# Moving the head transposes of the first attention block, its bias-table loads and its stored-value loads

## The chip, the cores and the metric

The kernel runs on one core of a Trainium2 chip. The metric is device microseconds of one execution, from the first instruction to the last result; 1697.91 us is the median of three runs of the kernel before (1692.98, 1697.91 and 1699.44).

## The reference

Two transformer blocks on one sequence of 512 tokens, 1024 features wide, each with a mixer and a feed-forward part. The part that the change touches is the first block's mixer, which adds two branches: an RWKV branch (a recurrence over the tokens) and a sparse attention with 8 heads in 2 key groups. Cut to that attention:

```python
q = rmsnorm(q.reshape(b, s, G, R, dh), q_norm_g) * (dh ** -0.5)
kc = rmsnorm(compress_blocks(k_c, ...), k_norm_g)          # 31 compressed keys
p_c = masked_softmax(einsum(q, kc) + bias_c, dist_c >= 0)  # compressed branch
o_cmp = einsum(p_c, vc)
# selected branch: rmsnorm(k_s); n_sel = min(16, 8 blocks): every causal block is selected
sc = einsum(q, k_sel) + bias; p = masked_softmax(sc, mask); o_slc = einsum(p, v_sel)
# window branch: rmsnorm(k_w), a window of 512 tokens
# output = gate_c * o_cmp + gate_s * o_slc + gate_w * o_win, then a projection,
# a sigmoid gate per feature, and the same for the RWKV branch
```

Queries and keys are normalised head by head, so a head's values must all be there, squared, summed and scaled, before they can be used. The second block has another attention (top-k over index scores) and a mixture of experts behind it.

## The kernel before

Everything is float32 with inputs in four tiles of 128 tokens. An exact product is made of three matmuls of rounded parts, hi by hi, hi by lo and lo by hi (`mm3`, L252). `wload` (L257) brings a 256 KB piece of a weight from memory on SP's queue (`raw`, 4 buffers), rounds it on ACT (`hi`, 3 buffers) and takes the rest on POOL or DVE (`lo`, 3 buffers).

A framework records the program and places the instructions of each engine in an order of its own, from the program order, the data that they need and the buffers of the pools; within an engine they then run strictly in that order. So the code's order is a wish: a transposition written behind a projection may already stand inside the next one.

`lin_a` (L268) projects the four token tiles at once, with weights as the moving operand: 8 steps of 128 features, 12 matmuls each, in four PSUM tiles (`pslin` twice, `pspr` twice). It takes a function `mid`, which is recorded once more than half of the steps are through. `lin_heads` (L1076) calls it and then normalises per head: ACT scales and squares, DVE sums, takes the reciprocal root in a row of small steps, and multiplies (the tiles are `hd` for keys, `hq` and `q` for queries). `lin_b` (L285) is the other form, weights stationary, 128x512 outputs; its rows are called dense below.

The first block's mixer is `block1`. After the RWKV recurrence come the gate products of tiles 8 to 15 (`gates`), then `nsa_in`: compressed keys and values, the RWKV output (`rwkv_out`, which ends in the tiles `obh`, `obl`), the q projection, the transposition of q's heads into `qT`, and for c = 0 (selected) and c = 1 (window) a projection of keys, values and gate (`w_kv`) and the transposition of two key groups into `kT`. Then `nsa_pair` runs four times, for one head of each group, called A and B: the compressed branch (scores in `CA`/`CB`, exponential on ACT, sums on DVE, four transposes, a product with `vc`), and two full branches: scores QK into `psA`/`psB` (two buffers each), bias and minimum on DVE (`NA`, `mnA`), exponential on ACT (`PA`), scaling by one over the sum on DVE, 10 transposes per head and products with `V`. The bias comes from a table `TB` per head (`toeplitz`, four DMAs on SP each). Work without that dependence fills the gaps: `proj_b` (dense, `obh`, `obl`, with `mb` made on DVE), `gates(range(8))` and behind them `merge`.

In the second block, `dsa_in` calls `lin_heads` for q and k, with `mid` for the transposition of q inside k's projection and of k inside v's, while DVE searches the top-k of the scores (`dsa_topk`); `dsa_pair` then runs its attention with heads A and B in step.

Of the kernel before, what the change touches and what calls it, by code (L numbers as in the profile page):

```python
# [10 lines left out]
F32 = mybir.dt.float32  # L11
F32R = mybir.dt.float32r
# [4 lines left out]
ALU = mybir.AluOpType  # L17
AX = mybir.AxisListType

T = 512  # L20
D = 1024
NT = 4
# [174 lines left out]
class Kern:  # L197
# [70 lines left out]
    def lin_a(self, pieces, h, N, consume, mid=None):  # L268
        ps = [self.pt("lin"), self.pt("lin"), self.pt("pr"), self.pt("pr")]
        kt, last = 0, sum(p.shape[-1] // N for p in pieces) - 1  # L270
        for p in pieces:
            hi, lo = self.wload(p)
            for j in range(p.shape[-1] // N):
                for t in range(NT):
                    c = slice(t * 128, (t + 1) * 128)
                    self.mm3(ps[t][:, :N], (h[0][:, kt, c], h[1][:, kt, c]),
                             (hi[:, j * N:(j + 1) * N], lo[:, j * N:(j + 1) * N]), kt == 0, kt == last)
                kt += 1
            if mid and kt > last // 2:
                mid()  # L280
                mid = None
        for t in range(NT):
            consume(t, ps[t])
# [126 lines left out]
    def block1(self):  # L410
        nc, tc, I = self.nc, self.tc, self.I
        with ExitStack() as s1:
            self.gt = s1.enter_context(tc.tile_pool(name="gt", bufs=1))
            self.thd = self.dr.tile([16, 128, T], F32, name="thd")
            self.bvd = self.dr.tile([4, 128, T], F32, name="bvd")
            self.ynd = self.dr.tile([NT, 2, 128, 256], F32, name="ynd")
            with tc.tile_pool(name="rw", bufs=1) as rw:
                self.rw = rw
                with tc.tile_pool(name="rwp", bufs=1, side="right") as rp:
                    self.rp = rp  # L420
                    with tc.tile_pool(name="nrm", bufs=1, side="right") as nrm, tc.tile_pool(name="btab", bufs=1) as bt:
                        self.rwkv_open(nrm, bt)
                    self.load_cc(rw, "cc1")
                    self.rwkv_in()
                    with tc.tile_pool(name="rwm", bufs=1, side="right") as rm:
                        self.rm = rm
                        for b in range(2):
                            for hp in range(2 * b, 2 * b + 2):
                                self.X[hp] = self.rwkv_col(hp, rw)
                                self.X[8 + hp] = self.rwkv_col(8 + hp, rw)  # L430
                                self.rwkv_prep(hp)
                            for t in range(NT):
                                self.rwkv_batch(t, b, ("A", "B", "pr")[(4 * b + t) % 3])
                        self.gates(range(8, 16))
            mx = s1.enter_context(tc.tile_pool(name="mx", bufs=1))
            self.mx = mx
            self.obT = (mx.tile([128, 4, T], F32R, name="obh"), mx.tile([128, 4, T], F32R, name="obl"))
            self.nsa_in()
            if self.stop == "nsa_in":
                return  # L440
            self.mb = s1.enter_context(tc.tile_pool(name="mbp", bufs=1)).tile([128, 8, T], F32, name="mb")
            with tc.tile_pool(name="att", bufs=1) as at:
                self.at = at
                for i in range(4):
                    pso = self.pt()
                    self.nsa_pair(i, pso)
                    self.split(pso, self.oaT[0][:, i, :], self.oaT[1][:, i, :])
                    self.dump("oaT", self.oaT[0][:, i, :].bitcast(F32), (slice(None), i))
                self.proj_b()
                self.gates(range(8))  # L450
            self.xs = self.rstack.enter_context(tc.tile_pool(name="xs", bufs=1, side="right"))
            self.x = self.xs.tile([128, NT, D], F32, name="x")
            nc.scalar.dma_start(self.x, I["x"].rearrange("(t p) d -> p t d", p=128))
            self.mtp = s1.enter_context(tc.tile_pool(name="mtp", bufs=1))
            self.merge()
            self.h_open("fg")
            self.ss = self.out_proj(I["w_o1"], self.mT, after=self.h_half)
            self.dump("x1", self.x)

    def nsa_in(self):  # L460
        nc, tc, I, mx = self.nc, self.tc, self.I, self.mx
# [9 lines left out]
        qs = mx.tile([128, 1], F32, name="qs")  # L471
        self.stt(qs, self.pc("qg"), -0.125, self.pc("kg"), ALU.mult, ALU.mult)
        self.load_cc(mx, "cc5")
        with tc.tile_pool(name="cmp", bufs=1) as cp:
# [59 lines left out]
                    self.split(pv, self.kcT[0][:, :, 0:31], self.kcT[1][:, :, 0:31], scale=qs)  # L534

            qt = self.lin_heads(cp, [I["w_q"][j] for j in range(8)], 512, 8)
            q2 = cp.tile([128, NT, 8, 2, 64], F32R, name="q2", tag="w1", bufs=1)
            for t in range(NT):
                self.split(qt[t], q2[:, t, :, 0], q2[:, t, :, 1])
            for h in range(8):  # L540
                ps = self.pt("AB"[h % 2])
                for t in range(NT):
                    self.tr(ps[:, t * 128:(t + 1) * 128], q2[:, t, h].rearrange("p j d -> p (j d)").bitcast(F32))
                self.copy("av"[h % 2], self.qT[:, h, :], ps)
            for c in range(2):

                def extra(t, ps):
                    self.copy("a", self.V[:, t, c, :], ps[:, 128:256])
                    self.act(self.gate[:, 3 - t, 12 * c:12 * c + 12], ps[:, 256:268], AF.Tanh, scale=0.5)

                kt = self.lin_heads(cp, [I["w_kv"][4 * c + j] for j in range(4)], 268, 2, extra, dup=True)
                for g in range(2):
                    ps = self.pt("AB"[g])
                    for t in range(NT):
                        self.tr(ps[:, t * 128:(t + 1) * 128], kt[t][:, g].rearrange("p j d -> p (j d)"))
                    self.split(ps, self.kT[0][:, c, g, :], self.kT[1][:, c, g, :], scale=qs)
            self.ts(self.gate, self.gate, 0.5, 0.5)

    def softmax_min(self, N, ps, tb, mn):
        self.nc.vector.tensor_tensor_reduce(out=N, in0=ps, in1=tb, scale=1.0, scalar=3.0e38,  # L560
                                            op0=ALU.add, op1=ALU.min, accum_out=mn)

    def nsa_pair(self, i, pso):
        nc, at = self.nc, self.at
# [2 lines left out]
        TB = []  # L567
        for g in range(2):
            h, tg = i + 4 * g, tl(g)
            tb3 = tg([128, 1, 896], "TB", 1)  # L570
            self.toeplitz(self.tab1, h, tb3)
            tb = tb3[:, 0, :]
            TB.append(tb)
            ps = self.pt("AB"[g])
            for t in range(NT):
# [391 lines left out]
    def rwkv_out(self):  # L967
        nc, tc = self.nc, self.tc
        with tc.tile_pool(name="rwo", bufs=1) as ro:
            bv = ro.tile([128, 4, T], F32, name="bv")  # L970
            nc.sync.dma_start(bv, self.bvd.rearrange("h p t -> p h t"))
            g2 = ro.tile([128, 512], F32, name="g2")
            nc.sync.dma_start(g2, self.I["g2"])
            mu1 = ro.tile([128, 1], F32, name="mu1b")
            self.ts(mu1, self.pc("mu", 13), -1.0, 1.0)
            ps = self.lin_b(self.I["w_rw"][13], self.h)
            x = ro.tile([128, T], F32, name="xl13")
            self.act(x, ps, AF.Identity, scale=mu1)
            self.stt(x[:, 1:], ps[:, :T - 1], self.pc("mu", 13), x[:, 1:], ALU.mult, ALU.add)
            self.act(x, x, AF.Tanh, scale=0.5)  # L980
            self.ts(x, x, 0.5, 0.5)
            for hp in range(4):
                yn = ro.tile([128, NT, 128], F32, name="yn", tag="yn", bufs=2)
                nc.sync.dma_start(yn, self.ynd[:, hp // 2, :, hp % 2 * 128:hp % 2 * 128 + 128].rearrange("t p c -> p t c"))
                ps = self.pt("A")
                for t in range(NT):
                    self.tr(ps[:, t * 128:(t + 1) * 128], yn[:, t, :])
                o = ro.tile([128, T], F32, name="otmp", tag="otmp", bufs=2)
                self.act(o, ps, AF.Identity, scale=self.pc("lg", hp), bias=self.pc("lb", hp))
                self.tt(o, o, bv[:, hp, :], ALU.add)  # L990
                ps = self.pt("B")
                self.mm(ps, g2[:, hp * 128:(hp + 1) * 128], x)
                self.tt(o, ps, o)
                self.split(o, self.obT[0][:, hp, :], self.obT[1][:, hp, :])
                self.dump("obT", o, (slice(None), hp))
# [722 lines left out]
```

## Time and profile before

| | us |
|---|---|
| median of three runs | 1697.91 |
| the profiled execution | 1697.58 |
| its span on the core | 1695.8 |
| PE busy | 1579.2 (93%) |
| DVE busy | 951.0 (56%) |
| ACT busy | 558.1 (33%) |
| mean granted TensorE clock | 0.955 |

The span runs from the first to the last instruction. Matmuls overlap, so PE counts as busy also where it runs at the lower of its two clocks: a granted clock of 1.00 is 2.4 GHz, 0.50 is 1.2 GHz, and a number between them is the mean over a stretch. Of the span, 384 to 640 us is the first block's projections and attention, 1110 to 1180 us the second block's projections, and the experts of the second block end it, behind loads from memory.

### The profile page before, as it was taken

How to read it: one execution, taken by the hardware profiler on the slowest of the kernel's cores; microseconds unless marked ns; L12 is line 12 of the kernel's file. 1: busy time of each engine (PE TensorE's matmuls, PEld its weight loads, DVE VectorE, ACT ScalarE, POOL GpSimd, SP SyncE). 2: the span in 40 equal slices, each digit the busy share in tenths (PEclk: the TensorE clock that was granted, in tenths of full speed). 3: DMA queues.
4: the chain of work that ended last, by engine and by line, in shares of the span. 5: the costliest groups of instructions: out<-in, count | busy, mean ns of one | idle time of the engine just before them, and what ended most of it. 6: DMA issues, size and time to landing. Idle time of an engine off the chain costs nothing. (4 is left out here: it accounts for less than half of the span.)

```text
span 1695.8 us, 25436 instructions
## 1 busy us (share of the span) xinstructions
PE 1579.2 (93%) x9595; PEld 1145.5 (68%) x9595; DVE 951.0 (56%) x2344; ACT 558.1 (33%) x1127; POOL 292.0 (17%) x232
## 2 busy tenths in 40 slices
PE   7999999998899999999999999989888996899995
PEld 5678787868566577888888888677666475465431
DVE  5566866136587542777777333798488635343310
ACT  3432322325244433444444232434333431011010
POOL 4510101523110144000000000132032031121111
PEclk8899999999799999999999999999999997899898
DMA  5110111632222253223333333423211368899995
GB/s 188 62 57 16 57 55 51 211 102 64 80 74 66 87 166 89 87 95 93 100 93 94 93 94 104 100 75 95 69 38 38 144 229 308 282 403 401 403 393 186
DMA packets 90760, 230.74 MB, mean 136 GB/s; under 512 B 16015, under 2 KB 20527, under 8 KB 82156
## 3 DMA queue, kind: packets, MB, share of 16 engines
q1 hardware_dynamic: 76608, 203.29, 35.2%
q0 software_dynamic: 4736, 11.14, 2.7%
q10 hardware_dynamic: 9292, 14.66, 2.6%
q8 instruction: 77, 1.26, 0.3%
q14 instruction: 47, 0.39, 0.1%
HBM read 217.49 MB, written 21.04 MB: 141 GB/s over the span
## 5 line engine op out<-in xcount | busy, mean ns | idle before, releaser
L227 ACT ACTIVATE hi<-raw 128x512 fp32r<-128x512 f32 (+1 forms) x314 | 197.4, 631 | 434.5 <-PE pslin L246 186.1
L215 POOL TENSOR_TENSOR lo<-raw,hi 128x512 fp32r<-128x512 f32 (+1 forms) x152 | 198.6, 1310 | 601.7 <-ACT hi L227 499.7
L246 PE MATMUL pslin<-hhi,hi 128*128 128x512 f32 x696 | 281.5, 404 | 3.4 <-ACT hi L227 3.4
L246 PE MATMUL pslin<-hhi,lo 128*128 128x512 f32 x696 | 281.3, 404 | 2.2 <-POOL lo L215 2.2
L246 PE MATMUL pslin<-hlo,hi 128*128 128x512 f32 x696 | 281.9, 405 | 0.0
L215 DVE TENSOR_TENSOR lo<-raw,hi 128x512 fp32r<-128x512 f32 x162 | 111.3, 687 | 121.0 <-ACT hi L227 120.0
L246 PEld LDWEIGHTS pslin<-hhi,lo 128*128 128x128 f32 x696 | 132.3, 190 | 38.1 <-issue 4.1
L246 PEld LDWEIGHTS pslin<-hhi,hi 128*128 128x128 f32 x696 | 132.5, 190 | 35.6 <-ACT hi L227 4.3
L246 PEld LDWEIGHTS pslin<-hlo,hi 128*128 128x128 f32 x696 | 132.6, 190 | 32.5 <-issue 3.1
L246 PE MATMUL psA<-gu,XT 128*64 128x512 f32 x512 | 144.6, 626 | 3.4 <-DMA gu<-in_egu_dram 3.4
L246 PEld LDWEIGHTS psA<-gu,XT 128*64 128x64 f32 x512 | 56.5, 144 | 67.2 <-issue 46.4
L246 PE MATMUL psB<-dn,hT 128*64 128x512 f32 x256 | 70.9, 600 | 1.0 <-ACT hT L209 1.0
L218 DVE SCALAR_TENSOR_TENSOR u<-lr,pcol,u 128x511 f32<-128x511 f32 x88 | 65.9, 749 | 8.2 <-ACT u L227 6.6
L212 POOL CAST spread<-sprf 128x1280 fp32r<-128x1280 f32 x1 | 1.3, 1256 | 384.1 <-DMA sprf<-in_spread_dram 384.1
L215 DVE TENSOR_TENSOR lr<-pslin,Rb 128x512 f32<-128x512 f32 x54 | 37.3, 690 | 50.6 <-PE pslin L246 44.7
L246 PE MATMUL pslin<-lo,hhi 128*128 128x512 f32 (+1 forms) x144 | 55.1, 383 | 2.8 <-DVE lo L215 2.8
L246 PE MATMUL pspr<-hi,hhi 128*128 128x512 f32 (+1 forms) x144 | 55.1, 385 | 1.2 <-ACT hq L227 1.2
L246 PE MATMUL pslin<-hi,hhi 128*128 128x512 f32 (+1 forms) x144 | 56.0, 390 | 0.0
L246 PE MATMUL pspr<-lo,hhi 128*128 128x512 f32 (+1 forms) x144 | 54.6, 379 | 0.0
L246 PE MATMUL pslin<-hi,hlo 128*128 128x512 f32 (+1 forms) x144 | 54.2, 376 | 0.0
L246 PE MATMUL pspr<-hi,hlo 128*128 128x512 f32 (+1 forms) x144 | 54.0, 375 | 0.0
L246 PEld LDWEIGHTS psB<-dn,hT 128*64 128x64 f32 x256 | 27.7, 139 | 31.7 <-issue 16.1
(660 smaller groups left out, 3098.3 us busy)
## 6 DMA issues: line engine op xcount, KB each, us to landing
gu<-in_egu_dram SPq DMA_DIRECT2D x64, 1024.0 KB, 16.6
dn<-in_ed_dram SPq DMA_DIRECT2D x64, 512.0 KB, 17.2
raw<-in_w_up_dram SPq DMA_DIRECT2D x88, 256.0 KB, 2.6
raw<-in_w_dn_dram SPq DMA_DIRECT2D x44, 256.0 KB, 2.6
raw<-in_w_g_dram SPq DMA_DIRECT2D x32, 256.0 KB, 2.7
raw<-in_w_o_dram SPq DMA_DIRECT2D x32, 256.0 KB, 2.8
raw<-in_w_a_dram SPq DMA_DIRECT2D x32, 256.0 KB, 2.7
raw<-in_w_rw_dram SPq DMA_DIRECT2D x28, 256.0 KB, 2.7
```

The costliest lines, as they stand in the source:

```text
L212: return self.nc.gpsimd.tensor_copy(out, in_)
L215: return (eng or self.nc.vector).tensor_tensor(out, a, b, op=op)
L218: return self.nc.vector.scalar_tensor_tensor(out, a, s, b, op0=op0, op1=op1)
L227: return self.nc.scalar.activation(out, in_, f, **k)
L246: return self.nc.tensor.matmul(out, lhsT=lhsT, rhs=rhs, start=start, stop=stop)
```

## The change

Four things are done.

1. `lin_a` records `mid` after 6 of 8 steps, where it was after more than half. This holds for the second block's two uses too.
2. In `nsa_in` q's transposition becomes a function that is `mid` of the first key projection, the first keys' transposition is `mid` of the second one, and the second keys' transposition follows two gate products, `gates(range(2))`, which are taken from behind the attention.
3. The bias tables are loaded by `bias_pair`, one pair ahead, in two pools in turn; pair 0's are recorded ahead of `nsa_in`.
4. `rwkv_out` loads the stored values `bv` in four pieces of 256 KB, each with its pair, in two buffers, where it was one load of 1 MB.

```diff
@@ lin_a
-            if mid and kt > last // 2:
+            if mid and kt > 3 * last // 4:
                 mid()
@@ block1
+            self.TB = [[], []]
+            self.bias_pair(0)
             self.nsa_in()
...
                 self.at = at
+                self.bias_pair(1)
                 for i in range(4):
                     pso = self.pt()
                     self.nsa_pair(i, pso)
+                    self.bias_pair(i + 2)
...
                 self.proj_b()
-                self.gates(range(8))
+                self.gates(range(2, 8))
@@ nsa_in
             qt = self.lin_heads(cp, [I["w_q"][j] for j in range(8)], 512, 8)
+            def turn_q():
+                q2 = ...            # split and 32 transposes into qT, as before
+            def turn_k(c):
+                for g in range(2):
+                    ps = self.pt("AB"[g])
+                    for t in range(NT):
+                        self.tr(ps[:, t * 128:(t + 1) * 128], kt[c][t][:, g].rearrange("p j d -> p (j d)"))
+                    self.split(ps, self.kT[0][:, c, g, :], self.kT[1][:, c, g, :], scale=qs)
+            kt = []
             for c in range(2):
...
-                kt = self.lin_heads(cp, [I["w_kv"][4 * c + j] for j in range(4)], 268, 2, extra, dup=True)
-                for g in range(2):
-                    ...
+                kt.append(self.lin_heads(cp, [I["w_kv"][4 * c + j] for j in range(4)], 268, 2, extra, dup=True,
+                                         mid=(lambda: turn_k(0)) if c else turn_q))
+            self.gates(range(2))
+            turn_k(1)
@@ new function
+    def bias_pair(self, i):
+        if i < 4:
+            for g in range(2):
+                pool = self.at if i % 2 else self.mx
+                tb = pool.tile([128, 1, 896], F32, name="TB" + "AB"[g], tag="TB" + "AB"[g], bufs=1)
+                self.toeplitz(self.tab1, i + 4 * g, tb)
+                self.TB[g].append(tb)
@@ nsa_pair
-            tb3 = tg([128, 1, 896], "TB", 1)
-            self.toeplitz(self.tab1, h, tb3)
-            tb = tb3[:, 0, :]
+            tb = self.TB[g][i][:, 0, :]
@@ rwkv_out
-            bv = ro.tile([128, 4, T], F32, name="bv")
-            nc.sync.dma_start(bv, self.bvd.rearrange("h p t -> p h t"))
...
             for hp in range(4):
+                bv = ro.tile([128, T], F32, name="bv", tag="bv", bufs=2)
+                nc.sync.dma_start(bv, self.bvd[hp])
...
-                self.tt(o, o, bv[:, hp, :], ALU.add)
+                self.tt(o, o, bv, ALU.add)
```

What the order of the built program makes of it, at three places.

PE, the second keys' transposition (`hd`) in the kernel before: it stands behind 18 dense rows of `obh`/`obl` and is mixed with the compressed scores of pair 0 (`kcT`).

```order
L246 MATMUL pslin<-obl,hi 128x512
L246 MATMUL pslin<-obh,lo 128x512
L250 MATMUL psA<-cc,hd_4684 128x128
L250 MATMUL psB<-cc,hd_4684 128x128
L246 MATMUL psA<-kcT_3763,qT 128x32
L250 MATMUL psA<-cc,hd_4686 128x128
L250 MATMUL psB<-cc,hd_4686 128x128
L246 MATMUL psA<-kcT_3764,qT 128x32
```

The same on PE of the changed kernel.

```order
L246 MATMUL pslin<-hlo,hi 128x512
L246 MATMUL pslin<-hhi,lo 128x512
L250 MATMUL psA<-cc,hd_4700 128x128
L250 MATMUL psA<-cc,hd_4702 128x128
L250 MATMUL psA<-cc,hd_4704 128x128
L250 MATMUL psA<-cc,hd_4706 128x128
L250 MATMUL psB<-cc,hd_4700 128x128
L250 MATMUL psB<-cc,hd_4702 128x128
```

Now 24 matmuls of the key projection and 48 dense rows of two gate products (`hhi`, `hlo`) stand between the first keys' transposition and this one, and the eight transposes stand together. The first keys' transposition itself stands behind 72 of the second projection's 96 matmuls, where it stood behind 32. The 32 transposes of q have hardly moved: 72 matmuls of the first projection stand ahead of them, where there were 70.

ACT, from the second keys' copies into `kT` to pair 0's compressed branch, in the kernel before.

```order
L227 ACTIVATE kT_3759<-psA,qs 128x512
L227 ACTIVATE kT_3759<-psB,qs 128x512
L227 ACTIVATE hi<-raw 128x512 x3
L227 ACTIVATE CA<-CA 128x124
L209 ACTIVATE CTA<-psA 31x512
L227 ACTIVATE PA,smA<-NA,mnA 128x128
```

The same on ACT of the changed kernel.

```order
L227 ACTIVATE kT_3769<-psA,qs 128x512
L227 ACTIVATE kT_3769<-psB,qs 128x512
L227 ACTIVATE CA<-CA 128x124
L227 ACTIVATE CB<-CB 128x124
L227 ACTIVATE hi<-raw 128x512
L209 ACTIVATE CTA<-psA 31x512
L209 ACTIVATE CTB<-psB 31x512
L227 ACTIVATE PA,smA<-NA,mnA 128x128
L227 ACTIVATE PB,smB<-NB,mnB 128x128
```

Three weight roundings `hi` stood ahead of the exponential of `CA`; now both exponentials come first.

PE, the compressed branch and the first scores of pair 0, in the kernel before: A alone, B's stand 23 rows later.

```order
L250 MATMUL psA<-cc,CA 31x128 x4
L246 MATMUL psA<-kT_3759,qT 128x256
L246 MATMUL psA<-kT_3760,qT 128x256
L246 MATMUL pspr<-CTA,vc 64x512
L246 MATMUL psA<-kT_3759,qT 128x256
L246 MATMUL psA<-kT_3760,qT 128x256
```

The same on PE of the changed kernel.

```order
L250 MATMUL psA<-cc,CA 31x128 x4
L250 MATMUL psB<-cc,CB 31x128 x4
L246 MATMUL psA<-kT_3769,qT 128x256
L246 MATMUL psA<-kT_3770,qT 128x256
L246 MATMUL pspr<-CTA,vc 64x512
L246 MATMUL pspr<-CTB,vc 64x512
L246 MATMUL psB<-kT_3769,qT 128x256
L246 MATMUL psB<-kT_3770,qT 128x256
```

A and B now go in step in pairs 0, 2 and 3, with 12 dense rows in one block behind the scores of a branch; pair 1 keeps A ahead of B. In the second block the transposes of q and of k stand 24 matmuls later in the next projection. On SP the eight table loads of pair 0 stand behind the store of the last RWKV values (`ynd`), ahead of `rwkv_out`'s loads, and the last two `yn` and `bv` loads behind later weight loads. POOL's order is the same.

## Rows read from the trace of the kernel before

**Rows 1.** Busy time by stretch (engines, granted clock, DMA share), first block
```profile
390.00:440.00 50.00, 42.88 (x256) 39.11 (x256) 27.91 (x65) 18.46 (x54) 13.05 (x10) 0.86 0.29 83
440.00:484.00 44.00, 38.44 (x177) 24.87 (x176) 27.82 (x97) 16.32 (x46) 3.83 (x3) 0.84 0.24 69
484.00:590.00 106.00, 101.81 (x508) 66.77 (x507) 74.44 (x254) 49.05 (x135) 11.66 (x9) 0.98 0.21 68
590.00:640.00 50.00, 46.66 (x190) 36.21 (x190) 20.27 (x24) 17.38 (x30) 22.78 (x18) 0.97 0.50 158
```

**Rows 2.** PE's timeline: rows with idle time (start, duration, [idle <-releaser])
```profile
395.41 0.33 PE L250 MATMUL psA<-cc,q 128*128 128x128 f32 x1 [2.47 <-DVE q L215]
...
410.63 0.33 PE L250 MATMUL psA<-cc,hd 128*128 128x128 f32 x1 [2.26 <-DVE hd L215]
...
426.24 0.40 PE L250 MATMUL psA<-cc,hd 128*128 128x128 f32 x1 [2.39 <-DVE hd L215]
...
444.06 1.03 PE L250 MATMUL psA<-cc,CA 128*31 128x128 f32 x4 [3.32 <-issue]
...
451.88 0.80 PE L246 MATMUL pslin<-obh,hi 128*128 128x512 f32 x1 [1.69 <-DVE mb L218]
...
591.23 0.51 PE L246 MATMUL pslin<-hhi,hi 128*128 128x512 f32 x1 [1.21 <-ACT hi L227]
```

**Rows 3.** Busy time by stretch, around the second keys' transposition
```profile
430.00:435.00 5.00, 5.00 (x16) 4.13 (x16) 1.69 (x4) 0.63 (x1) 0.80 (x1) 0.50 0.78 218
435.00:440.00 5.00, 5.00 (x20) 4.00 (x19) 0.60 (x2) 0.63 (x1) 1.78 (x2) 0.84 0.30 107
```

**Rows 4.** PE's timeline: spacing of projection matmuls and of dense rows
```profile
412.08 0.29 PE L246 MATMUL pslin<-hi,hhi 128*128 128x268 f32 x1
...
419.50 0.39 PE L246 MATMUL pslin<-obh,hi 128*128 128x512 f32 x1
...
423.46 0.39 PE L246 MATMUL pslin<-obh,lo 128*128 128x512 f32 x1
```

**Rows 5.** DVE's timeline: normalised keys, and pair 0's compressed branch
```profile
425.75 1.43 DVE L215 TENSOR_TENSOR hd<-hq,rsy 128x256 f32<-128x256 f32 x4
...
435.19 0.44 DVE L215 TENSOR_TENSOR CA<-CA,cmA 128x124 f32<-128x124 f32 x1
441.44 1.25 DVE L215 TENSOR_TENSOR CA<-CA,cc 128x124 f32<-128x124 f32 x1 [5.81 <-ACT CA L227]
...
443.67 0.29 DVE L215 TENSOR_TENSOR CA<-CA,csA 128x124 f32<-128x124 f32 x1
```

**Rows 6.** ACT's timeline ahead of pair 0's compressed branch
```profile
440.58 0.63 ACT L227 ACTIVATE hi<-raw 128x512 fp32r<-128x512 f32 x1 [2.15 <-PE pslin L246]
441.12 0.29 ACT L227 ACTIVATE CA<-CA 128x124 f32<-128x124 f32 x1
```

**Rows 7.** PE's timeline: second block, transposes of q and of k
```profile
1135.31 0.33 PE L250 MATMUL psA<-cc,hq 128*128 128x128 f32 x1 [3.17 <-DVE hq L215]
...
1162.63 0.33 PE L250 MATMUL psA<-cc,hq 128*128 128x128 f32 x1 [2.66 <-DVE hq L215]
```

**Rows 8.** Busy time by stretch, second block's projections
```profile
1130.00:1140.00 10.00, 6.83 (x31) 5.48 (x30) 9.86 (x29) 2.43 (x5) 1.44 (x2) 0.83 0.21 54
...
1160.00:1170.00 10.00, 7.10 (x31) 6.02 (x32) 9.62 (x28) 3.42 (x6) 1.26 (x1) 0.83 0.18 52
```

**Rows 9.** DVE's timeline: the weight remainders behind the second block's top-k
```profile
1173.09 0.69 DVE L215 TENSOR_TENSOR lo<-raw,hi 128x512 fp32r<-128x512 f32 x1 [0.44 <-ACT hi L227]
...
1180.48 1.41 DVE L215 TENSOR_TENSOR lo<-raw,hi 128x512 fp32r<-128x512 f32 x2 [1.77 <-ACT hi L227]
```

**Rows 10.** PE's timeline: second block's attention, heads A and B in step
```profile
1320.06 1.58 PE L250 MATMUL psA<-cc,PA 128*128 128x128 f32 x8 [2.38 <-DVE PA L223]
...
1334.40 1.53 PE L250 MATMUL psA<-cc,PA 128*128 128x128 f32 x8 [0.67 <-DVE PA L223]
```

**Rows 11.** SP's timeline: table load of pair 0, head A (issue)
```profile
428.54 1.74 SPq L408 DMA_DIRECT2D TBA<-vtab_relb  x4
```

More of the change, by code (lines that the diff above doesn't have):

```diff
@@ L536, in nsa_in @@
             qt = self.lin_heads(cp, [I["w_q"][j] for j in range(8)], 512, 8)
[L537 to L541, printed above, removed]
-                for t in range(NT):
-                    self.tr(ps[:, t * 128:(t + 1) * 128], q2[:, t, h].rearrange("p j d -> p (j d)").bitcast(F32))
-                self.copy("av"[h % 2], self.qT[:, h, :], ps)
+            def turn_q():
+                q2 = cp.tile([128, NT, 8, 2, 64], F32R, name="q2", tag="w1", bufs=1)
+                for t in range(NT):
+                    self.split(qt[t], q2[:, t, :, 0], q2[:, t, :, 1])
+                for h in range(8):
+                    ps = self.pt("AB"[h % 2])
+                    for t in range(NT):
+                        self.tr(ps[:, t * 128:(t + 1) * 128], q2[:, t, h].rearrange("p j d -> p (j d)").bitcast(F32))
+                    self.copy("av"[h % 2], self.qT[:, h, :], ps)
+            def turn_k(c):
+                for g in range(2):
+                    ps = self.pt("AB"[g])
+                    for t in range(NT):
+                        self.tr(ps[:, t * 128:(t + 1) * 128], kt[c][t][:, g].rearrange("p j d -> p (j d)"))
+                    self.split(ps, self.kT[0][:, c, g, :], self.kT[1][:, c, g, :], scale=qs)
+            kt = []
             for c in range(2):
@@ L549, in extra @@
                     self.act(self.gate[:, 3 - t, 12 * c:12 * c + 12], ps[:, 256:268], AF.Tanh, scale=0.5)
-                kt = self.lin_heads(cp, [I["w_kv"][4 * c + j] for j in range(4)], 268, 2, extra, dup=True)
-                for g in range(2):
[L553 to L556, printed above, removed]
+                kt.append(self.lin_heads(cp, [I["w_kv"][4 * c + j] for j in range(4)], 268, 2, extra, dup=True,
+                                         mid=(lambda: turn_k(0)) if c else turn_q))
+            self.gates(range(2))
+            turn_k(1)
             self.ts(self.gate, self.gate, 0.5, 0.5)
```

## The prediction

> **What bounds the kernel now.** I read the busy times by stretch first. From 390 to 640 us [rows 1] PE is busy 42.88 of 50 us, 38.44 of 44, 101.81 of 106 and 46.66 of 50: it idles 20.2 us in all, and no other engine comes near it there (DVE 27.91, 27.82, 74.44 and 20.27 us). So time goes in two ways: PE stands still, or it runs at the lower clock. The last figures but two of these rows give the second: a mean granted clock of 0.86, 0.84, 0.98 and 0.97 costs one minus that, times the stretch, which is 7.0, 7.0, 2.1 and 1.5 us, 17.6 in all (a little too much, since an idle slow PE loses nothing). A stretch thus holds 14.1, 12.6, 6.3 and 4.8 us that a better order could give back, 38 in sum.
>
> PE's timeline then says who ends the idle times. Three are transposes that come before their heads are normalised: q's at 395.41 (2.47 us, released by DVE), the selected keys' at 410.63 (2.26) and the window keys' at 426.24 (2.39) [rows 2]. Behind the last the clock stays low for ten microseconds: 0.50 and then 0.84 [rows 3], which is 2.5 + 0.8 = 3.3 us, and with the slow matmuls from 426.24 to 430 about 4.9 (an estimate). Then pair 0's compressed branch: 3.32 at 444.06 and 1.69 at 451.88, in a stretch at clock 0.84 [rows 1, 2].
>
> The 3.32 is put down to "issue", so the chain must be followed back. DVE had the shifted scores `CA` ready at 435.19 + 0.44 = 435.63, and its next step waited 5.81 us for ACT's exponential [rows 5]. ACT did that at 441.12, right behind a weight rounding of 440.58, which had itself waited for PE to free a buffer [rows 6]. The exponential needed nothing but its turn: 5.5 us lost to queueing, of which the dense rows on PE covered a part.
>
> In the second block the same pattern stands twice, with a difference: the transposes of q and k wait 3.17 and 2.66 us for DVE [rows 7], and there DVE is busy 9.86 and 9.62 of 10 us [rows 8], with the top-k search, so DVE and not PE may set the pace.
>
> What lies behind both stretches moves with them: the feed-forward part is PE's own, and the experts' loads begin when their tokens are known. I let a gain pass to the end one for one.
>
> **The change, part by part.** Sums are made against the profiled run of 1697.58 us, which is 0.3 below the median of the runs.
>
> *q's transposes.* 72 instead of 70 matmuls ahead, at (419.50 - 412.08) / 60 = 0.124 us each [rows 4]: 0.25 us more cover for a wait of 2.47. The change hardly does here what it says. Value 0.2, between 0 and 0.5.
>
> *Selected keys' transposes.* 72 instead of 32 matmuls of the next projection ahead: 40 x 0.124 = 5.0 us of cover for a wait of 2.26 [rows 2]. It goes: 2.3, and nothing is late behind it, as the transposes need only DVE.
>
> *Window keys' transposes.* The chain from the end of their projection (419.50, where dense rows begin [rows 4]) to the last `hd` (425.75 + 1.43 = 427.2 [rows 5]) is 7.7 us. Before, 18 dense rows covered (423.46 - 419.50) / 17 = 0.233 each, 4.2 us; now it is 48, 11.2 us, so 3.5 us are spare. The idle 2.39 goes, and with it what the clock fell for: 4.9. Value 7.3, between 2.4 (the clock falls elsewhere) and 7.3. Two gate products are not extra work: 48 dense rows leave the end of the attention. Their weights' roundings stand on ACT behind the keys' squares, but only from the third piece on, which PE needs 24 x 0.233 = 5.6 us after the projection; ACT is through with the squares about 1.5 us after it (an estimate from 16 rows of 0.2 to 0.4 us in the same place). So no new wait.
>
> *Pair 0.* The exponentials no longer stand behind roundings. The chain from the scores to the scaled `CA` without the queue is about 1.1 us for three DVE steps (an estimate from the last one's 0.44), 0.3 for the exponential, and 441.44 to 443.96 on DVE [rows 5, 6], some 4 us; with B interleaved on DVE perhaps 6. Now 21 dense rows, 4.9 us, and B's scores, 0.9, stand before the transposes. I leave 2 us idle, where 44 - 38.44 = 5.56 stood [rows 1], and no long slow stretch. Two scaled branches in step cost 0.9 each (below). So the 12.6 us of this stretch become 3.8: a gain of 8.8, bounded by 3 (idle time gone, clock not) and 11.
>
> *A and B in step.* The trace has no such pair in the first block; the nearest rows are in the second, where PE waited for the scaled `PA` 2.38 and 0.67 us [rows 10] with fewer dense rows to cover. Now 12 dense rows, 2.8 us, stand there, so I go by the smaller and add a little: 0.9 us for each of six branches. For the four in pairs 2 and 3 this is 3.6, pair 1 stays at about 1.9, and I add 3 us of slow clock, where the stretch lost 6.3: 2.2 worse. Ends: 4 better (the cover suffices everywhere) and 20 worse (third rival).
>
> *End of the attention.* 49 instead of 104 dense gate rows stand there, and the 1.21 us for a rounding behind a waiting gate [rows 2] with its slow clock (1.5) may go: value 1, between -1 and 2.8.
>
> *Tables and stored values.* The eight table issues cost SP time (1.74 us for four [rows 11]), not PE; nothing waited for them in the trace. Earlier, they stand ahead of weight loads. Value 0, between -2 and 0. The stored values are the same bytes in four pieces: 0, between -1 and 0.5.
>
> First block: 0.2 + 2.3 + 7.3 + 8.8 - 2.2 + 1 = 17.4.
>
> *Second block.* The two waits are 3.17 + 2.66 us, and the clock behind them, 0.83 in both stretches, costs 1.7 each: 9.2 [rows 7, 8]. The transposes now have 24 x 0.233 = 5.6 us more cover, so PE could gain all of it. But DVE has no free time, and the next thing that PE needs, the weight remainders `lo` at 1173.09 and 1180.48, stand on DVE behind the top-k steps [rows 9]. PE arrives earlier and waits there; the waits of 0.44 and 1.77 us on ACT show that DVE is ahead again only by then. I take half, 4.6, between 1 and 9.2.
>
> Sum 22.0: 1697.58 - 22.0 = 1675.6, set against the median 1676.
>
> **A rule that speaks against it.** In the trace a short idle time does not always cost the clock: after 2.26 us at 410.63 the matmuls from 412.08 on keep their 0.124 us [rows 2, 4], after 2.39 us at 426.24 it fell [rows 2, 3]. The Trainium skill, "TensorE: Matmul & The Clock Gate", section "A second HAM failure mode: psum-queue depth-cycling", tells of a kernel in which short pauses between groups of matmuls, as PSUM tiles are cycled through, make the clock fall and rise over and over. Scores in step, with two buffers a head, are such a pattern. What it would do here is the first rival, priced from rows.
>
> **The rivals.**
> 1. *The waits go, the clock doesn't come back.* In step, PE would pause often and briefly, and fall again. For it: 0.67 to 2.38 us pauses in the second block's attention [rows 10]. Against: the dense rows between. Then only idle time is won: 0.2 + 2.3 + 2.4 + 3 - 1.3 + 1 = 7.6 in the first block, where the -1.3 is the idle 106 - 101.81 = 4.2 of pairs 1 to 3 less my 3.6 + 1.9, and 2.9 in the second: 10.5, so 1687.
> 2. *DVE keeps the gain.* In step, DVE has to do both heads' minimum, scaling and copies before PE goes on, and top-k holds the second block. For it: DVE is busy 74.44 of 106 us in the attention [rows 1]. Against: 30% of it is free. Pair 0 then gives 3 instead of 8.8 and the second block 0.5: 22 - 5.8 - 4.1 = 12.1, so 1686.
> 3. *Slower: each branch in step waits as the worst row does.* Six branches at 2.38 us idle [rows 10] and 1.7 us of clock [rows 8] are 24.5, instead of 5.4 + 3 in my sum: 16.1 worse; with rival 2's second block (4.1 less) and half of pair 0's gain lost to the same wait (4.4) it is 22 - 24.6, so 1700. For it: rows of this very form. Against: 12 dense rows that those lack. It decides from about 3.7 us a branch.
> 4. *All of it.* The second block gives 9.2, and pairs 1 to 3 gain 3 instead of losing 2.2: 22 + 4.6 + 5.2 = 31.8, so 1666.
>
> **Chances.** My forecast 0.50, rival 1 0.14, rival 2 0.12, rival 3 0.10, rival 4 0.08, and 0.06 for no change that can be told, if the order moves the waits rather than removes them. About 0.5%, 8.5 us, is what a measurement of this kernel can tell from no change. Rivals 1 and 2 stand near that bound and give a quarter of theirs, 0.065, to "same"; of rival 3 half is within it. So same 0.065 + 0.05 + 0.06, 0.17, slower 0.05, faster 0.78. The range of 1662 to 1692 holds the forecast with its bounds, rivals 1, 2 and 4, and leaves out rival 3 and most of no change. The forecast's own range is 1669 to 1683.
>
> **What would show it.** Right, if the transposes of both keys follow matmuls without idle time, the clock is 1.00 from the second key projection to pair 0, the exponential of `CA` follows its scores within 1 us, and q's wait of about 2.3 us is still there. The step on branches is right if PE waits about 1 us for `PA` in pairs 0, 2 and 3, and the second block's if PE has no wait at the transposes, and one for `lo` that it hadn't. Wrong, if the granted clock of 484 to 590 falls well below 0.98, if PE waits over 3 us in a branch, if weights of the two moved gate products come late, or if the feed-forward part and the experts don't begin earlier by what the two blocks gained.

## The result and the profile after

The changed kernel takes 1678.60 us (median of six runs, 1672.11 to 1682.97), the kernel before on the same chip 1693.71 us (six runs, 1692.98 to 1699.44): a ratio of 0.990 (0.991 between the medians), 95% interval 0.9881 to 0.9919. The forecast was 1676 us, a gain of 22 us; measured are 15 us between the medians and 19.4 us between the two profiled executions (1697.58 and 1678.15 us). The one profiled before was 3.9 us above its median of six, and so was the median of three that the forecast started from (1697.91).

The same work can be found in both traces, so the gain can be read along the way:

| mark, on PE | before | after | difference |
|---|---|---|---|
| RWKV recurrence, first step | 139.9 | 142.9 | +3.0 |
| compressed keys, first product | 347.3 | 351.8 | +4.5 |
| q's first transposition | 395.4 | 399.9 | +4.5 |
| first product behind the mixer | 633.5 | 612.7 | -20.8 |
| second block, transposes of `z` (inputs of its linear attention) | 1209.0 | 1188.2 | -20.8 |
| second block, last mask product of its attention (`mB`) | 1359.2 | 1341.5 | -17.7 |
| end of the span | 1695.8 | 1676.3 | -19.5 |

From q's transposes to the end of the first mixer 25.3 us were won (17.4 forecast). The second block's projections gave 0.0 (4.6 forecast), the part behind them, up to that mask product, lost 3.1. The 3.0 us up to 139.9 lie in code that is the same in both; the 1.5 between there and 347.3 belong to the change.

Busy time by stretch in the changed kernel, columns as in [rows 1]: time, busy PE, PEld, DVE, ACT, POOL, then the granted clock, DMA share and GB/s.

```profile
390.00:440.00 50.00, 47.44 (x322) 42.83 (x322) 36.23 (x88) 23.10 (x65) 19.64 (x14) 1.00 0.34 110
440.00:484.00 44.00, 41.77 (x214) 27.62 (x212) 33.47 (x114) 21.70 (x63) 6.04 (x5) 1.00 0.26 81
484.00:590.00 106.00, 99.69 (x521) 70.72 (x520) 66.44 (x224) 46.99 (x125) 18.39 (x15) 1.00 0.23 78
590.00:640.00 50.00, 47.47 (x208) 37.12 (x208) 24.55 (x33) 17.07 (x31) 21.33 (x17) 1.00 0.43 133
```

The clock column has gone from 0.86, 0.84, 0.98 and 0.97 [rows 1] to 1.00 throughout: the 17.6 us that the lower clock cost are all back in this profile. Idle time of PE is 2.56, 2.23, 6.31 and 2.53 us, 13.6 in sum, where 20.2 stood. So some two thirds of the gain is clock, although every edit was aimed at a wait. The stretches are the same times in both kernels and not quite the same work, so the sum is firmer than its parts.

This profile is the best of its kind. Four more ran PE through the first block's mixer in the same order: the changed kernel once more (`after_again`) and three experiments below that edit the second block alone. From q's transposes to the end of the mixer they take 213.6 (`after_again`), 213.6 (`old_mid2`), 214.6 (`lo_pool`) and 215.5 us (`gl_loads`), against 212.8 here, and each has ten microseconds at a granted clock of 0.83, which cost 1.7 us: from 510 us in the first two, from 400 in `lo_pool`, from 450 in `gl_loads`. Against the one profile before, the first block thus gave 22.6 to 25.3 us.

PE's timeline of the changed kernel, rows with idle time:

```profile
399.92 0.33 PE L250 MATMUL psA<-cc,q 128*128 128x128 f32 x1 [2.22 <-DVE q L215]
...
485.06 0.55 PE L250 MATMUL psA<-cc,PA 128*128 128x128 f32 x3 [0.58 <-DVE PA L223]
498.82 0.55 PE L250 MATMUL psA<-cc,PA 128*128 128x128 f32 x3 [0.94 <-DVE PA L223]
...
535.76 0.55 PE L250 MATMUL psA<-cc,PA 128*128 128x128 f32 x3 [0.85 <-DVE PA L223]
```

q's wait is still there (2.22 us). No wait stands at either keys' transposes or at `CA`, where [rows 2] had 2.26, 2.39 and 3.32. The branches in step wait 0.58 to 0.94 us for `PA` (up to 0.98 for `PB`), close to the 0.9 of the forecast. On ACT the exponentials now follow their scores:

```profile
432.85 0.69 ACT L227 ACTIVATE kT<-psB,qs 128x512 fp32r<-128x512 f32 x1
435.56 0.31 ACT L227 ACTIVATE CA<-CA 128x124 f32<-128x124 f32 x1 [2.02 <-DVE CA L215]
435.77 0.29 ACT L227 ACTIVATE CB<-CB 128x124 f32<-128x124 f32 x1
```

ACT waits for DVE's `CA`, where in [rows 5, 6] DVE waited 5.81 us for ACT.

### The profile page after: what moved, and what is told of

It reads as the page before. It is cut to its first block, busy times and chain, and to the rows that moved or that the text cites. A ratio compares the mean times of both kernels' runs of the same rounds, so it can differ in the third digit from the quotient of the medians.

```text
span 1676.3 us, 25429 instructions
## 1 busy us (share of the span) xinstructions
PE 1561.4 (93%) x9591; PEld 1133.2 (68%) x9595; DVE 955.1 (57%) x2344; ACT 557.0 (33%) x1127; POOL 294.8 (18%) x232
## 5 line engine op out<-in xcount | busy, mean ns | idle before, releaser
L227 ACT ACTIVATE th<-psA,rs 128x256 f32<-128x256 f32 x16 | 7.6, 474 | 123.9 <-PE psA L246 123.9
```

The lines of the kernel that those rows point to most:

```text
L227: return self.nc.scalar.activation(out, in_, f, **k)
```

## Experiments in the first block

Ratios are against the kernel before, run on the same chip.

**One half of the change each.** Without `bias_pair`, the split `bv` and the new threshold:

```diff
-            if mid and kt > 3 * last // 4:
+            if mid and kt > last // 2:
...    no bias_pair; tables in nsa_pair, bv in one load, as before
```

> The kernel before with the new transposition functions and the two gate products ahead of the second keys' transposition; mid is still recorded after half of the steps, the tables and stored values are loaded as before. Theory: the two key waits (2.26 and 2.39 us before) are gone and the clock no longer falls behind them, while pair 0 keeps A ahead of B and its exponential stands behind roundings: 7 to 11 us less than before, 0.9935 to 0.996. Rival 1 (tables make the gain, by bringing A and B in step): no more than the two idle times, 0.997 to 1.000. Rival 2 (both parts are needed, since the clock falls at the next short wait anyway): idle times gone, granted clock of the stretch 390 to 480 us still below 0.9, 0.997.

And the kernel before with only the tables and stored values changed:

```diff
+            self.bias_pair(0)
             self.nsa_in()
...    bias_pair(1), bias_pair(i + 2) and bv per pair as in the change
```

> The kernel before with the tables loaded a pair ahead and the stored values in four pieces; transposes and gate products as before. Theory: waits of 2.2 to 2.4 us before both keys' transposes stay and the clock falls behind the second; the exponentials of pair 0 follow their scores, so its 3.3 and 1.7 us go; the early loads cost some 1 us near 320 us: 4 to 8 us less than before, 0.995 to 0.998. Rival 1 (tables make the whole gain): 0.990 to 0.992. Rival 2 (the key order makes it all): 1.000 to 1.002.

Measured: 0.9956 (0.9939 to 0.9973) and 0.9957 (0.994 to 0.9974). Both theories of a single cause fall: each half gives about 7.5 us, together the 15 of the whole change. In the traces, from q's transposes to the end of the mixer, they give 14.5 and 11.4 us, together 25.9, close to the 25.3 of the whole change. (Both profiled executions were the slowest of their six and reach q's transposes about 5.5 us later than the profile before, which is why their spans show less.) What each left behind shows in PE's timeline, first with the transposes alone:

```profile
418.17 0.33 PE L250 MATMUL psA<-cc,hd 128*128 128x128 f32 x1 [1.09 <-DVE hd L215]
...
450.36 0.60 PE L250 MATMUL psA<-cc,CA 128*31 128x128 f32 x4 [3.31 <-issue]
...
457.97 0.80 PE L246 MATMUL pslin<-obh,hi 128*128 128x512 f32 x1 [2.06 <-DVE mb L218]
```

then with the tables alone:

```profile
416.05 0.33 PE L250 MATMUL psA<-cc,hd 128*128 128x128 f32 x1 [2.29 <-DVE hd L215]
...
431.63 0.33 PE L250 MATMUL psA<-cc,hd 128*128 128x128 f32 x1 [2.39 <-DVE hd L215]
```

The waits at pair 0 go with the tables; with the transposes the window keys' wait goes, and of the selected keys' 2.26 us 1.09 are left, against the expectation. Only with the new threshold are they gone too, which is what the threshold gives in the first block, beside 0.24 us at q (2.46 here, 2.22 in the changed kernel). The stored values in four pieces were not tried alone. The tables do it through the order: wherever they are loaded ahead, A and B stand in step in pair 0 and both exponentials ahead of the next rounding. With the transposes alone the exponential stands behind a rounding, as before (ACT's timeline):

```profile
446.89 0.63 ACT L227 ACTIVATE hi<-raw 128x512 fp32r<-128x512 f32 x1 [2.15 <-PE pslin L246]
447.43 0.29 ACT L227 ACTIVATE CA<-CA 128x124 f32<-128x124 f32 x1
```

**The changed kernel without `bias_pair`.**

```diff
-            tb = self.TB[g][i][:, 0, :]
+            tb3 = tg([128, 1, 896], "TB", 1)
+            self.toeplitz(self.tab1, h, tb3)
+            tb = tb3[:, 0, :]
...    and no calls of bias_pair
```

> The changed kernel with the tables loaded inside each pair as before; all else of the change stays. Theory: as with the transposition functions alone, plus an earlier-than-needed cover for the first keys, minus the cost of the early loads near 320 us: 0.993 to 0.996, and PE waits about 3 us for pair 0's compressed branch at most. Rival 1 (tables make the gain): 0.998 to 1.000. Rival 2 (tables are neutral): 0.989 to 0.991.

Measured 0.9924 (0.9906 to 0.9942), between theory and rival 2. PE waits 3.32 us at `CA` again, the granted clock from 440 to 484 us is 0.88, and the stretch from q to the mixer's end is 5.9 us longer than in the changed kernel (3.2 longer than in the slowest profile of its order); the two profiled spans differ by 0.8 us only (1677.1 and 1676.3), since 2.9 us lie the other way before q, 2.5 of them in code that is the same, and 2.3 behind the mixer. Between this kernel and the changed one the runs decide nothing.

**The two gate products back behind the attention.**

```diff
-            self.gates(range(2))
             turn_k(1)
...
-                self.gates(range(2, 8))
+                self.gates(range(8))
```

> The changed kernel with all eight gate products behind the attention again, so that the second keys' transposition follows its projection with 18 dense rows between. Theory: PE waits 2.4 us there again and the clock falls behind it for some ten microseconds, as before: 5 to 9 us more than the changed kernel, 0.993 to 0.996. Rival (the fall behind that wait was chance, as the clock stayed up behind the first keys' wait): only the 2.4 us come back, 0.991 to 0.992, with a granted clock of 1.00 from 420 to 440 us.

Measured 0.9936 (0.9912 to 0.9961). PE's wait for the window keys is 2.38 us, and the clock behind it:

```profile
420.00:430.00 10.00, 7.62 (x38) 6.42 (x37) 7.95 (x23) 2.32 (x4) 1.97 (x2) 0.81 0.39 119
430.00:440.00 10.00, 10.00 (x44) 7.39 (x44) 5.36 (x24) 4.17 (x15) 2.54 (x2) 0.85 0.41 132
```

It falls as in [rows 3], which costs 3.4 us in these 20. Wait and clock together are 5.8 us, of the 7.3 of the forecast for this step. That q to the mixer's end takes 7.4 us more than in the changed kernel (4.7 to 7.4 over the five profiles of its order) is not all this step's: 1.7 of it is a granted clock of 0.89 from 525 to 540 us, at a wait of 1.71 us for `PB`. The rival (the fall was chance) has three profiles against it: the wait of 2.4 us for the window keys stands in the kernel before, with the tables alone and here, and the clock fell behind it each time.

**A gate product ahead of the first key projection**, to cover q:

```diff
             qt = self.lin_heads(cp, [I["w_q"][j] for j in range(8)], 512, 8)
+            self.gates(range(1))
...
-            self.gates(range(2))
+            self.gates(range(1, 2))
             turn_k(1)
```

> The changed kernel with the first of the two gate products put ahead of the first key projection, and the second left where it is: 24 dense rows (5.6 us) more between the q projection and q's transposes, 24 fewer ahead of the second keys'. Theory: q's wait of 2.2 us is gone, the second keys' chain of 7.7 us is still covered by 24 projection matmuls and 24 dense rows (8.6 us), and the clock cannot fall at q: 2 to 4 us less than the changed kernel, 0.9865 to 0.989. Rival (the wait only moves on, to the second keys' transposes or pair 0): 0.990.

Measured 0.9927 (0.9911 to 0.9943). The rival was right on the mechanism (the time came out above its 0.990). q's wait is gone, and the window keys' transposes wait again, with the clock falling to 0.83 from 430 to 440 us. I had counted 24 projection matmuls as cover that belong to the window keys' own projection: between its end (421.88 us) and the transposes only 24 dense rows stand, 5.6 us, and the chain to the last `hd` (430.48) takes 8.6, not 7.7. PE's waits:

```profile
428.46 0.33 PE L250 MATMUL psA<-cc,hd 128*128 128x128 f32 x1 [1.01 <-DVE hd L215]
...
429.87 1.00 PE L250 MATMUL psA<-cc,hd 128*128 128x128 f32 x3 [1.08 <-DVE hd L215]
```

**Tables later.**

```diff
-            self.bias_pair(0)
             self.nsa_in()
...
+            self.bias_pair(0)
             qt = self.lin_heads(cp, [I["w_q"][j] for j in range(8)], 512, 8)
```

> The changed kernel with pair 0's bias tables loaded just ahead of the q projection instead of ahead of everything in the attention's input stage. Theory: PE no longer waits 0.5 to 2.3 us near 320 to 330 us for weights that stood behind the tables on SP, and nothing else moves: 1 to 2 us less, 0.988 to 0.990, with PE busy all of 300 to 340 us. Rival (those waits come from the split stored-value loads or the late gate weight alone): the waits stay, 0.990.

Measured 0.9906 (0.9885 to 0.9927): the time alone cannot tell it from the changed kernel. PE's busy time from 300 to 345 us can: 44.22 of 45 us in the changed kernel, 44.84 here, 45.00 before. SP's timeline of the changed kernel has the cause, and ACT's the consequence:

```profile
306.68 1.73 SPq L408 DMA_DIRECT2D TBA<-vtab_relb  x4
308.44 0.49 SPq L408 DMA_DIRECT2D TBB<-vtab_relb  x1
310.08 0.34 SPq L696 DMA_DIRECT2D thd<-gth  x1
318.06 0.36 SPq L261 DMA_DIRECT2D raw<-in_w_g_dram  x1
```

```profile
320.75 0.63 ACT L227 ACTIVATE hi<-raw 128x512 fp32r<-128x512 f32 x1 [4.53 <-DMA raw<-in_w_g_dram]
```

The table loads stand ahead of a gate weight, beside a 2 MB load on ACT's queue; the weight is issued at 318.06 us (309.64 before), and PE waits at 327.47 for what is made of it. The marks agree: from the last step of the RWKV recurrence to the compressed keys it is 75.7 us before, 77.3 in the changed kernel (77.9 in its second profile) and 76.0 here, so the early tables cost about 1.3 us, as the theory had it. Without any early table (`no_tables`) it is 76.8, so the other edits, or chance, have a share.

## Experiments in the second block

**The old threshold there.**

```diff
-            if mid and kt > 3 * last // 4:
+            if mid and kt > (3 * last // 4 if self.nsa_mid else last // 2):
...    nsa_mid is True in nsa_in, from the q projection to the second key projection, and False elsewhere
```

> The changed kernel with the second block's two transposes recorded after half of the steps again; the first block keeps the change. Theory (DVE, with the top-k, sets the pace there, so that the moved transposes gave nothing): the waits of 2.7 to 3.2 us before both transposes come back, the new waits for the weight remainder and for ACT (1.33, 1.30 and 1.17 us) go, and from the first matmul behind the first mixer to the scan inputs z of the second block it takes 575.5 us as in both kernels, within 1; the time is that of the changed kernel, 0.988 to 0.992. Rival (the later transposes were worth the 4.6 us that were forecast, and something else took them): 4 to 5 us longer there, 0.992 to 0.995.

Measured 0.9897 (0.9877 to 0.9916). The waits of 3.17 and 2.66 us come back, and the way from the first mixer to `z` takes 574.9 us, against 575.5 in the changed kernel and in the one before: between these profiles PE saves both waits for nothing. In the changed kernel it waits elsewhere:

```profile
1118.60 0.33 PE L250 MATMUL psA<-cc,hq 128*128 128x128 f32 x1 [1.34 <-DVE hq L215]
...
1131.03 0.50 PE L246 MATMUL pspr<-hi,hhi 128*128 128x512 f32 x1 [1.33 <-ACT hq L227]
...
1158.39 0.50 PE L246 MATMUL pslin<-hhi,lo 128*128 128x512 f32 x1 [1.30 <-DVE lo L215]
1162.14 0.50 PE L246 MATMUL pslin<-hhi,hi 128*128 128x512 f32 x1 [1.17 <-ACT hi L227]
```

What was not expected stands behind it, at `z`. The changed kernel, then the one before:

```profile
1188.20 3.48 PE L246 MATMUL pspr<-cc,z 128*128 128x128 f32 x16 [2.49 <-DVE z L218]
```

```profile
1209.02 2.02 PE L246 MATMUL pspr<-cc,z 128*128 128x128 f32 x16 [2.50 <-DVE z L218]
```

The same wait, and after it 16 transposes at the lower or the higher clock. Over all profiles in which nothing else was changed there, six of each threshold, the way to `z` is 573.9 to 575.5 us with the new one (mean 574.4) and 574.4 to 575.8 with the old (575.3), and from `z` to the last mask product 151.3 to 153.5 (152.7) and 148.8 to 151.9 (150.0). So the new threshold gains 0.9 us ahead of `z` and loses 2.7 behind it: in the second block it costs about 1.8 us by these means.

**Weight remainders on POOL.**

```diff
                     self.dsa_topk(ix, acc)
-                    self.lo_eng = None
...    and in gla, behind the four query and key products:
+        self.lo_eng = None
```

> The changed kernel with the weight remainders of the second block's four query and key products made on POOL instead of DVE. Theory: PE arrives there 2 to 3 us earlier than it can go on, because the remainders stand behind top-k steps on DVE; on POOL they are free, so the wait of 1.30 us for them goes, and the stretch up to z becomes 1.5 to 4 us shorter: 0.987 to 0.9895. Rival (ACT's rounding and its buffers set the pace, as the wait of 1.17 us on ACT suggests): at most 0.5 us, 0.990.

Measured 0.9917 (0.9898 to 0.9935); to `z` 575.2 us, and from the last transposition of k to `z` 41.0, against 40.2 in the changed kernel. The rival was right: the wait for the remainder is gone, and the one for ACT's rounding grows from 1.17 to 1.92 us.

**Three loads off ACT's queue.** ACT's timeline of the changed kernel shows why the roundings are late:

```profile
1160.07 0.33 ACTq L235 DMA_DIRECT2D cc<-in_cc_dram  x1
1160.44 0.45 ACTq L1240 DMA_DIRECT2D glw<-in_glw_dram  x1
1160.92 0.44 ACTq L1242 DMA_DIRECT2D glb<-in_glb_dram  x1
1161.46 1.68 ACT L227 ACTIVATE hi<-raw 128x512 fp32r<-128x512 f32 x3 [6.93 <-issue]
```

That the load `cc` waits for memory that the top-k gives back is read from the time of its issue, 1160.07 us: DVE's last top-k row is

```profile
1159.75 0.29 DVE L224 TENSOR_SCALAR mB<-acc 128x256 bf16<-128x256 f32 x1
```

which ends at 1160.04. The edit:

```diff
-                    self.load_cc(gl, "cc2")
+                    self.load_cc(gl, "cc2", nc.gpsimd)
...    glw and glb likewise
```

> The changed kernel with the three loads of the second block's linear attention (constants cc, glw and glb) issued on POOL's queue instead of ACT's. Theory: in the changed kernel the weight roundings at 1161.46 us stood on ACT behind the issue of the load cc, and that waited for memory that the last top-k step on DVE gave back at 1160.07 us; off ACT's queue the roundings come earlier, PE's wait of 1.17 us for them is gone, and the way from the first mixer to z is 1 to 2 us shorter, 573.5 to 574.5 us. Rival (the roundings wait for DVE's remainders to give back their buffers): 575.5 us as before. The whole time differs from the changed kernel's by less than runs can tell, 0.988 to 0.991.

Measured 0.9883 (0.986 to 0.9907). The wait for the rounding is gone: two roundings now stand ahead of the time at which DVE's last top-k row ends (1161.60 us in this run), so it was not the remainders' buffers that held them (the rival).

```profile
1156.00 0.62 ACT L227 ACTIVATE hi<-raw 128x512 fp32r<-128x512 f32 x1
...
1157.98 0.63 ACT L227 ACTIVATE hi<-raw 128x512 fp32r<-128x512 f32 x1 [1.36 <-PE pslin L246]
```

From the last transposition of k to `z` it takes 39.0 us, against 40.2 in the changed kernel and in four others with the new threshold (`no_tables`, the fifth, waits 2.9 us ahead of k's transposes instead): the theory's 1 to 2 us. Over the longer way from the mixer, 574.0 us, two profiles of the changed kernel themselves differ (575.5 and 573.9), so that number settles nothing.

## Two combinations

Tables late with the old threshold in the second block, and the same with `gates(range(1))` ahead of the first key projection and `gates(range(1, 3))` ahead of the window keys; beside them the changed kernel once more.

> The changed kernel with pair 0's tables loaded just ahead of the q projection and the second block's transposes recorded after half of the steps. Theory: both edits' gains add, 1 to 2 us near 320 us, and 3 to 4 us because the clock no longer falls at z: 4 to 6 us less than the changed kernel, 0.9865 to 0.9885, and the 16 transposes of z take 2.0 us, not 3.4. Rival (whether the clock falls at z is chance): the z transposes are slow again, 0.989 to 0.991.

> As the kernel before it in this call, with one gate product ahead of the first key projection and two ahead of the second keys' transposition. Theory: q's wait of 2.2 us is gone, and, unlike with one gate product each, the second keys' too, so that the clock stays up from 380 to 450 us: 2 to 3 us less than its neighbour, 0.985 to 0.987. Rival (the wait or the fall of the clock moves on to the first keys, pair 0 or a branch): no difference to its neighbour.

> The changed kernel as it is, on the chip of this call, for the comparison of its neighbours. Expected 0.988 to 0.992; PE waits 2.2 us at q's transposes, near 327 us for late weights, and the z transposes run at the lower clock. A theory that the clock's falls are chance expects z's transposes at full clock in about half of such profiles.

Measured 0.9875 (0.9854 to 0.9897), 0.988 (0.9859 to 0.9901) and 0.9892 (0.9866 to 0.9917): medians of 1675.27, 1676.17 and 1678.32 us. The first is 3 us ahead of the changed kernel, where 4 to 6 were expected, and these runs cannot tell it from no difference. The second is 0.9 us behind the first, where 2 to 3 less were expected: its rival's figure. In it q and both keys have no wait (PE is busy 49.70 of 50 us from 390 to 440), but the third gate product is missing behind the attention, where PE now waits longer for the merge (0.99 and 1.43 us in the changed kernel):

```profile
588.15 0.47 PE L246 MATMUL pslin<-oah,hi 128*128 128x512 f32 x1 [2.19 <-DVE mo L218]
...
610.24 0.50 PE L246 MATMUL pslin<-hi,mT 128*128 128x512 f32 x1 [1.68 <-DVE mo L218]
```

On the clock at `z` the profiles agree. The 16 transposes took 2.02 us in all six kernels with the old threshold in the second block (the one before, two of single halves, the old threshold alone and both combinations), and 2.84 to 3.61 us in all eight profiles with the new one.

## Why the prediction was right, and where not

The time was within the range and 2.6 us from the forecast, in part by luck. Three errors met: the first block gave 25.3 us instead of 17.4, the second nothing instead of 4.6, and 4.5 us were lost ahead of q's transposes, 3.0 of them in code that is the same in both. And the forecast started 4 us too high: over six runs each the gain is 15 us, not 22.

*q's transposes: right.* The wait is 2.22 us, as forecast. That the clock stayed up behind it was not forecast (it was 0.83 from 395 to 405 us before), and it was luck: of nine profiles with this wait the clock fell behind it in three (`lo_pool`, `tables_late` and the first combination), in `lo_pool` with PE's order unchanged.

*Selected and window keys: right in mechanism, about right in size.* No wait, clock 1.00; undoing the window keys' part brought back 5.8 us of wait and clock against 7.3. The chain took 8.6 us instead of 7.7 (420.25 to 428.88), so 2.4 us are spare before the transposes at 431.25, not 3.5. The stretch to 440 us gave 11.5 us (14.1 less the idle 2.56) against 9.8.

*Pair 0: right, a little small.* 12.6 us became 2.2, a gain of 10.4 against 8.8. What I had put down to the order of ACT came with the tables, as their half alone shows.

*A and B in step: mis-sized by the clock.* The idle time is 6.31 us, against 3.6 + 1.9 forecast. The 3 us of slow clock were not there: the stretch lost 6.3 before and 6.3 after, where I had 2.2 worse. In the second profile of the changed kernel the idle time is 5.70 us and the clock 0.98, 2.1 us: 1.5 worse. So the term lies between. The first rival did not come: with pauses of 0.6 to 1.0 us in the branches the clock was 1.00 for 106 us, and in the second profile it fell there once. The rule on short pauses in the Trainium skill ("TensorE: Matmul & The Clock Gate", section "A second HAM failure mode: psum-queue depth-cycling") stood for that rival; of the repeated falls that it tells of, the five profiles of this order show one at most in this stretch.

*End of the attention.* 4.8 us became 2.5 (1.00, idle 2.53): 2.3 against 1, within the bounds.

*Tables: within the bounds, not at the value.* 0.8 us of idle time near 320 us, and 1.5 on the way to the compressed keys, instead of 0.

*Second block: the step that failed.* I took half of 9.2 us. The waits did go, from 6.1 to 2.4 us at the transposes, but 3.8 us came back at three other places (1.33, 1.30 and 1.17): counted from the first product behind the mixer, DVE's last top-k row stands at 547 us, and at 545 before, so the full engine gave nothing. My lower bound of 1 us was too high (0.0 between these profiles, 0.9 in the mean of six and six). I had named DVE's `lo` as what PE would wait for. It is one of three: the other two are released by ACT, one by its work on `hq`, one by a weight rounding that stands on ACT's queue behind a load that waits for the top-k's memory. Of the clock that I counted as won (1.7 us at each transposition) nothing is left: at q's it still falls (0.83 from 1115 to 1125 us), and what k's gave (1.00 from 1145 to 1155) is lost at `z` (0.83 from 1185 to 1195), with about 3 us up to the last mask product of the attention, where I had let gains pass unchanged.

*Rivals.* Rival 2's second half (the second block gives 0 to 1) came true, its first half not. Rival 3 needed waits of 2.4 us in a branch; they are below 1. Rival 4 needed 9.2 us from the second block.

What stays open: why a wait of 2.2 to 2.5 us costs the clock in one place and not in another. In the second block the fall moved from k's transposes to `z` with the threshold, in all fourteen profiles; in the first block the same order had it at different places or not at all. No run here shows what decides it.

## What to carry to other kernels

Sum a stretch's losses as idle time plus one minus the granted clock; where the second is as large as the first, a wait that is left over can cost more than twice its length (here 2.4 us of wait and 3.4 us of clock behind it). When another engine is full, a wait removed ahead of it can come back behind it, as 3.8 us did here: look for the last thing that the full engine releases, memory included, and for the queues in which others stand behind that. A load issued early was not free on a shared queue (about 1.3 us here); see what it is put ahead of. And one profile per kernel is too few to price a term of a few microseconds: five of the same order differed by 2.7 us in one mixer.

## What was not expected of the hardware

A wait of 2.5 us ahead of the same 16 transposes was followed by the lower clock in eight of eight profiles with the new threshold and in none of six with the old. Behind q's wait of 2.2 us in the first block the same order of PE gave either. The first step of the RWKV recurrence, behind code that is the same in all kernels, began at 138.7 us in one profile and at 144.2 in another.
